# Eight narrow columns of a projection: one wide product per 512 tokens, or strips of 32 columns placed side by side

## The chip, the cores and the metric

The kernel runs on one core of a Trainium2 chip. The metric is the device time of one execution in microseconds. The engines are TensorE (PE in the profile; PEld is its weight load), VectorE (DVE), ScalarE (ACT), GpSimd (POOL) and SyncE (SP), which here issues nearly all DMAs. Each engine runs its own list of instructions in order; semaphores tie the lists together.

## The reference

One layer of a trunk over 2048 tokens of width 1024. The input is normalised and projected to four gated DeltaNet heads and four HGRN2 heads; their outputs are joined, projected, and followed by an MLP and a gated embedding term. What the change touches are eight columns of the projection: `a_gdn` and `b_gdn`, one of each per DeltaNet head.

```
hn = rms_norm(h, pre_mix_norm[i])
proj = jnp.einsum('btd,dc->btc', hn, w_in[i])
a_gdn = proj[..., OFF_GDN_A:OFF_GDN_B]          # 4 columns
b_gdn = proj[..., OFF_GDN_B:OFF_HG_F]           # 4 columns
beta = jax.nn.sigmoid(b_gdn)
g_dec = -jnp.exp(gdn_a_log[i]) * jax.nn.softplus(a_gdn + gdn_dt_bias[i])
o_a = gated_delta_rule_chunked(q_a, k_a, v_a, g_dec, beta)
```

The rule forms running sums of `g_dec` in each chunk and uses their exponentials, so a head needs the sums along the tokens as a row, and the sums and the gates as columns with one token per partition.

## The kernel before, in words

The mixer stage (39 to about 1010 us) works on four quarters of 512 tokens. x is held transposed, as eight tiles of 128 features by 512 tokens (`xt`), each scaled and then split into a high and a low part (`split`: ACT copies the rounded part, DVE subtracts). A product of x with 128 columns of weights, split likewise, is 24 matmuls of 128x128 by 128x512: high by high, high by low, low by high for each of eight k. The list `works` names the products in order. For each quarter it begins with the product `ab`, whose 128 columns hold the eight wanted ones (rows 0 to 3 and 32 to 35 of the result) and otherwise nothing that is used; then come eight products for each of four pairs of heads. `stage_work` loads the weights of a product three works ahead, `split_work` splits them two ahead, `keep_work` stores the split weights to memory in quarter 0, and the later quarters load them from there.

A product is three steps of eight matmuls. After each step a clock ticks, and the generators entered in an agenda (`at(time, generator, offsets)`) run on to their next yield. These issue the mixers' small work: `gdn_mixer` and `hgrn_mixer` of each head, `load_x` (loads, scalings and splits of the next quarter's x, in nine pieces during the nine steps before the boundary), and `decays`. PE's list is thus the program's order with the small matmuls at the ticks, SP's is by hand in the mixer loop, and the lists of ACT, DVE and POOL are set by a scheduler.

`decays` takes the result of `ab`. It evacuates four rows with a bias (L526) and four with a tanh (L527), forms the softplus by Exp and Ln of -|a| (L529 to L532; each of the two functions needs a table load on ACT), scales (L533) and forms the running sums in four scans (L535). It stores the sums to memory (L539), turns their order for odd chunks (L542), and transposes four tiles of 36 rows on PE (L546) into the columns `gcol`. Each DeltaNet head loads its own row of sums into `gf` (L638).

Around a boundary between quarters the list holds the end of the old quarter's heads: the last chunks of DeltaNet's recurrence (`psa` on PE, `r_g` on DVE, `psb` on PE, `w_g` on ACT, `psc` and `of_g` on PE, the new state `S_g` on DVE, and again `psa`), the HGRN head's `qk` on DVE and `hb` on ACT, and the next head's triangular system, a chain of short DVE operations `pr_g` and `xs_g`.

Quarter 0 is special: an embedding stage ahead of it (7 to 39 us) runs products `mme`, squares and their sums, and scales and splits the first x; ACT, DVE and SP have an order by hand there. `rsb_x` is the row of the inverse norms, spread over the partitions by DMA, that this scaling reads.

Of the kernel before, what the change touches and what calls it, by code (L numbers as in the profile page):

```python
# [10 lines left out]
F32 = mybir.dt.float32  # L11
# [4 lines left out]
ALU = mybir.AluOpType  # L16
# [4 lines left out]
P = 128  # L21
# [41 lines left out]
A_AHEAD = (-8, -6)  # L63


A_FIRST = (3, 7, 8, 8, 9, 10, 12, 14) + tuple(range(16, 24)) + (24, 26, 29, 32, 34, 36, 37)

A_LAST = (A_STEPS[:16] + (24, 25, 27, 28, 29, 30, 31) + tuple(range(32, 44))
# [28 lines left out]
def trunk(ctx, tc, x, xT, pT, vecs, w_in, w_ab, gdn_a_log, gdn_dt_bias, w_out, w_up, w_down,  # L97
# [30 lines left out]
    dec = cp.tile([4, 2], F32, name="dec")  # L128
# [15 lines left out]
    nexpa = cp.tile([4, 1], F32, name="nexpa")  # L144

    def vectors():

        ps = bank("ps_rows", pp)
        PE.transpose(ps[:, :N_ROWS], rows, ident[:N_ROWS, :N_ROWS])
        V.tensor_copy(cols, ps[:, :N_ROWS])  # L150
        V.tensor_scalar(ple_w, cols[:, R_PLE : R_PLE + KD], 0.5, None, ALU.mult)
        V.tensor_tensor(lb, lg, lg, ALU.subtract)
        S.activation(lb, lb, AF.Exp)
        V.reciprocal(lb1, lb)
        V.tensor_tensor(lb, lb, lb1, ALU.mult)
        V.tensor_tensor(lb, lb, lb, ALU.subtract)
# [3 lines left out]
        S.activation(nexpa, dec[:, 0:1], AF.Exp)  # L160
        V.tensor_scalar(nexpa, nexpa, -1.0, None, ALU.mult)

    mhalf = cp.tile([P, NC], F32, name="mhalf")
    V.memset(mhalf, -0.5)
# [220 lines left out]
    def half():  # L385

        for gen in agenda.pop(clock[0] - 0.5, ()):
            next(gen, None)

    with ExitStack() as ectx:  # L390
        es = ectx.enter_context(tc.tile_pool(name="es", bufs=1))
        with tc.manual_schedule(engines={mybir.EngineType.SP, mybir.EngineType.Activation, mybir.EngineType.DVE}):
# [9 lines left out]
            nc.sync.dma_start(dec[:, 0:1], gdn_a_log.rearrange("o h -> h o"))  # L402
            nc.sync.dma_start(dec[:, 1:2], gdn_dt_bias.rearrange("o h -> h o"))
# [39 lines left out]
            def put_x():  # L443
                k = len(xts[0])
                xts[0].append(operand(ra, None, f"xt0_{k}", raw=xraw[:, k]))
# [8 lines left out]
                done.append(d)  # L454
            while len(xts[0]) < KD:
                put_x()
            for f in stores:
                f()


    with mixers as mctx:
# [54 lines left out]

            return ready

        gb = mt("gb", "gb", 1, (36, QT))
        V.memset(gb, 0.0)  # L520

        def decays(ps, q):

            sp = m2.tile([4, QT], F32, tag="tmp", name=f"sp_{q}")
            se = m2.tile([4, QT], F32, tag="th", name=f"se_{q}")
            S.activation(sp, ps[0:4, :], AF.Identity, bias=dec[:, 1:2])  # L526
            S.activation(gb[32:36, :], ps[32:36, :], AF.Tanh, scale=0.5)  # L527
            V.tensor_scalar(gb[32:36, :], gb[32:36, :], 0.5, 0.5, ALU.mult, ALU.add)
            V.scalar_tensor_tensor(se, sp, -1.0, sp, ALU.mult, ALU.max)  # L529
            S.activation(se, se, AF.Exp, scale=-1.0)  # L530
            S.activation(se, se, AF.Ln, bias=1.0)
            V.scalar_tensor_tensor(sp, sp, 0.0, se, ALU.max, ALU.add)  # L532
            V.tensor_scalar(sp, sp, nexpa, None, ALU.mult)  # L533
            for c in range(NC):
                V.tensor_tensor_scan(gb[0:4, blk(c)], one[0:4, :], sp[:, blk(c)], 0.0, ALU.mult, ALU.add)  # L535
            gd = dr.tile([4, QT], F32, name=f"gd{q}")
            decay[q] = [gd, None]
            yield
            nc.sync.dma_start(gd, gb[0:4, :])  # L539
            yield  # L540
            back = mt(f"gbb_{q}", "gbb", 1, (36, QT // 2))
            V.tensor_copy(back.rearrange("p (n b i) -> p n b i", b=NB, i=SB), odd_back(gb))  # L542
            yield
            ps = bank(f"ps_gb_{q}", ph)
            for c in range(NC):
                PE.transpose(ps[:, c * 36 : (c + 1) * 36], back[:, blk(c // 2)] if c % 2 else gb[:, blk(c)],  # L546
                             ident[:36, :36])
            gcol = sm.tile([P, NC, 36], F32, tag="gcol", name=f"gcol_{q}", bufs=2)
            V.tensor_copy(gcol.rearrange("p c n -> p (c n)"), ps[:, : NC * 36])
# [83 lines left out]
        def gdn_mixer(q, h, live):  # L633
# [8 lines left out]
            beta = gcol[:, :, 32 + h : 33 + h].rearrange("p c o -> p (c o)")  # L642
            cd = sm.tile([P, NC], F32, tag="cd", name=f"cd_{n}")
            both = sm.tile([P, 2, NC], F32, tag="tail", name=f"tail_{n}")
            tail, eg = both[:, 0], both[:, 1]
# [372 lines left out]
                yield  # L1018
            at(t, once(), (0,))

        STEPS = SPT = 3
# [63 lines left out]
        def load_x(q):  # L1085

            rsb = spread_load(x_r[q], f"x{q}", m2, "rsx", 1)
            raws = {}

            def load(k):  # L1090
                raws[k] = m2.tile([P, QT], F32, tag="ld", name=f"raw_xt{q}_{k}", bufs=2)
                nc.sync.dma_start(raws[k], xT[blk(k), tok(q)])

            def scale(k):
                V.scalar_tensor_tensor(raws[k], raws[k], col(R_PREMIX + k), rsb, ALU.mult, ALU.mult)

            def ready(k):
                t = ra.tile([P, 2, QT], F32R, tag="ring", name=f"xt{q}_{k}")
                split(t, V, raws.pop(k))
                xts[q].append(t)  # L1100

            xts[q] = []
            for k in (0, 1):
                load(k)
            yield
            for k in (2, 4):
                t = wp.tile([P, 2, QT], F32, tag="raw", name=f"raw_xt{q}_{k}", bufs=2)
                nc.sync.dma_start(t, xT[k * P : (k + 2) * P, tok(q)].rearrange("(k p) t -> p k t", p=P))
                raws[k], raws[k + 1] = t[:, 0], t[:, 1]
            for k in (0, 1):  # L1110
                scale(k)
                ready(k)
                load(k + 6)
                yield
            for k in range(2, KD):
                scale(k)
                if k % 2:
                    yield
            for k in range(2, KD):
                ready(k)  # L1120
                if k % 2:
                    yield

        def down_sums(g):

# [14 lines left out]
                for k, n in enumerate(names):  # L1140
                    sumd[n, g] = c, k

        per_q = SPT * (1 + 8 * 4)
        starts = [per_q * q + 5 + n * i for q, m, n in ((1, 6, 14), (2, 5, 16), (3, 5, 16)) for i in range(m)]
        for g, t in enumerate(starts):
            at(t, down_sums(g), (0, 4, 6, 10))
        for q in range(1, NQ):
            at(per_q * (q - 1) + 30, x_scale(q), range(0, 22, 2))
            at(per_q * q, load_x(q), range(-9, 0))
            call(per_q * q, boundary)  # L1150
        for q in range(2):
            at(0, norm_steps(accs[q], 1.0 / D, EPS, f"e{q}", partial(ple_r.__setitem__, q)),
               [4 * q + i for i in (0, 2, 4, 5, 6)])
        with tc.manual_schedule(engines={mybir.EngineType.SP}):
            stage_work(0)
            stage_work(1)
# [3 lines left out]
            for j, (name, key, src, q, h, then, g, b) in enumerate(works):  # L1160
# [9 lines left out]
                for s in range(SPT):  # L1170
                    for i in range(s * nt // SPT, (s + 1) * nt // SPT):
                        if i == (2 * s + 1) * nt // (2 * SPT):
                            half()
                        PE.matmul(ps, *terms[i], start=i == 0, stop=i == nt - 1)  # L1174
                    if s == SPT - 1 and h is None:
                        at(clock[0], decays(ps, q), (0, 2, 3, 5) if q else (0, 2, 4, 7))
                    tick()
                    if s == SPT - 1 and h is not None:
                        then(ps, q, h, g, b)

            outs = early_outs()
# [801 lines left out]
```

## Time and profile before

| | us |
|---|---|
| median of 3 runs (2644.4 to 2645.62) | 2645.34 |
| the profiled execution | 2640.8 |
| its span, from first to last instruction | 2639.0 |
| PE busy in the span | 2602.0 |
| DVE busy | 1964.8 |
| ACT busy | 1466.0 |
| POOL busy | 137.0 |

The granted clock of TensorE was 1.000 throughout. A row of the timeline gives the start, the length, the engine, the line, the operation and its tiles; a square bracket behind it says how long the engine idled before it and which instruction ended the idling. The length of a matmul includes its way through the array, and matmuls overlap, so the distance between starts is their price. In a row of the windows stand, for each engine, the busy time and the count of instructions in that stretch, then the granted clock, the busy share of the DMA engines and the GB/s.

### The profile page before, as it was taken

How to read it: one execution, taken by the hardware profiler on the slowest of the kernel's cores; microseconds unless marked ns; L12 is line 12 of the kernel's file. 1: busy time of each engine (PE TensorE's matmuls, PEld its weight loads, DVE VectorE, ACT ScalarE, POOL GpSimd, SP SyncE). 2: the span in 40 equal slices, each digit the busy share in tenths (PEclk: the TensorE clock that was granted, in tenths of full speed). 3: DMA queues.
4: the chain of work that ended last, by engine and by line, in shares of the span. 5: the costliest groups of instructions: out<-in, count | busy, mean ns of one | idle time of the engine just before them, and what ended most of it. 6: DMA issues, size and time to landing. Idle time of an engine off the chain costs nothing.

```text
span 2639.0 us, 43910 instructions
## 1 busy us (share of the span) xinstructions
PE 2602.0 (99%) x15593; PEld 2143.6 (81%) x15593; DVE 1964.8 (74%) x4032; ACT 1466.0 (56%) x2991; POOL 137.0 (5%) x147
## 2 busy tenths in 40 slices
PE   8999999999999999999999999999999999999999
PEld 6787788878878888787888888888888888888887
DVE  7778777776777777579988778767877765478775
ACT  7665655465556555566666465555454465565331
POOL 0000000000000000110000000001000001101000
PEclk9999999999999999999999999999999999999999
DMA  8878777767767675774675576665644475677663
GB/s 279 288 243 263 255 270 247 239 221 248 244 201 251 224 235 163 225 214 138 215 234 183 179 234 224 213 212 186 224 145 168 140 245 186 202 252 251 209 219 128
DMA packets 267788, 573.87 MB, mean 217 GB/s; under 512 B 55578, under 2 KB 60152, under 8 KB 250416
## 3 DMA queue, kind: packets, MB, share of 16 engines
q1 hardware_dynamic: 265264, 566.86, 65.0%
q0 software_dynamic: 2304, 4.20, 0.9%
q8 instruction: 123, 2.02, 0.3%
q14 instruction: 97, 0.79, 0.1%
HBM read 410.57 MB, written 160.37 MB: 216 GB/s over the span
## 4 chain that ended last, share of the span: by engine, by line
PE 80%; DVE 7%; DMA 6%; ACT 3%; issue 3%; SPq 1%; POOL 0%; DVEq 0%; ACTq 0%; POOLq 0%
PE d L1208 23%; PE u L1208 23%; PE mm L1174 19%; PE mmg L1208 7%; PE mmo L1057 1%; PE mme L203 1%; DMA xs<-in_x_dram 1%; DMA ud_g<-u_g 1%; DMA cache_in<-w 1%; DMA sys_g<-ud_g 1%; DVE pr_g L744 1%; DVE xs_g L746 0%; DMA wd<-in_w_down_dram 0%; DVE xt L177 0%; PE psc_g L828 0%
## 5 line engine op out<-in xcount | busy, mean ns | idle before, releaser
L1174 PE MATMUL mm<-xt,w 128*128 128x512 f32 x3072 | 786.4, 401 | 2.9 <-DVE acc_vg L569 1.5
L1174 PEld LDWEIGHTS mm<-xt,w 128*128 128x128 f32 x3072 | 552.9, 188 | 109.0 <-ACT w L176 1.9
L1208 PE MATMUL d<-db,da 128*128 128x512 f32 x2688 | 612.9, 389 | 0.0
L1208 PE MATMUL u<-t,wu 128*128 128x512 f32 x2604 | 591.2, 389 | 0.0
L1208 PEld LDWEIGHTS d<-db,da 128*128 128x128 f32 x2688 | 504.5, 188 | 104.7
L1208 PEld LDWEIGHTS u<-t,wu 128*128 128x128 f32 x2604 | 488.8, 188 | 101.5
L230 DVE TENSOR_TENSOR db<-db 128x512 fp32r<-128x512 f32 x224 | 159.5, 712 | 60.6 <-ACT db L229 60.2
L1606 DVE TENSOR_TENSOR u<-u,u 128x512 f32<-128x512 f32 x224 | 150.0, 680 | 52.4 <-PE u L1208 50.9
L229 ACT ACTIVATE db<-db 128x512 fp32r<-128x512 f32 x224 | 141.0, 629 | 65.3 <-DMA db<-hid 60.8
L1208 PE MATMUL mmg<-h2T,wg 128*128 128x512 f32 (+1 forms) x792 | 174.7, 383 | 0.0
L1208 PEld LDWEIGHTS mmg<-h2T,wg 128*128 128x128 f32 x792 | 145.5, 188 | 29.1
L1649 ACT ACTIVATE u<-u 128x512 f32<-128x512 f32 x128 | 80.7, 631 | 152.8 <-DVE u L1606 152.2
L177 DVE TENSOR_TENSOR da<-da 128x512 fp32r<-128x512 f32 x128 | 93.9, 734 | 91.6 <-ACT da L176 91.3
L176 ACT ACTIVATE da<-da 128x512 fp32r<-128x512 f32 x128 | 80.6, 630 | 128.3 <-DMA da<-sumd 110.2
L1208 PE MATMUL mmo<-mixT,w_out 128*128 128x512 f32 x600 | 138.7, 391 | 3.3 <-DVE w_out L177 2.0
L1208 PEld LDWEIGHTS mmo<-mixT,w_out 128*128 128x128 f32 x600 | 112.2, 188 | 28.8 <-DVE w_out L177 3.2
L176 ACT ACTIVATE wu<-a 128x512 fp32r<-128x512 f32 x124 | 75.1, 623 | 54.8 <-DMA a<-in_w_up_dram 51.8
L177 DVE TENSOR_TENSOR wu<-a,wu 128x512 fp32r<-128x512 f32 x124 | 85.7, 694 | 8.8 <-ACT wu L176 8.3
L177 DVE TENSOR_TENSOR da<-dr,da 128x512 fp32r<-128x512 f32 x96 | 68.2, 711 | 22.5 <-ACT da L176 20.9
L1650 ACT ACTIVATE u<-u 128x512 f32<-128x512 f32 x128 | 80.4, 628 | 3.0
L176 ACT ACTIVATE da<-dr 128x512 fp32r<-128x512 f32 x96 | 60.5, 630 | 31.4 <-DMA dr<-in_w_down_dram 25.6
L246 POOL TENSOR_TENSOR acc_y<-acc_y,sq_y 128x512 f32<-128x512 f32 x28 | 37.8, 1349 | 759.4 <-ACT sq_y L245 759.4
(402 smaller groups left out, 3673.3 us busy)
## 6 DMA issues: line engine op xcount, KB each, us to landing
w<-cache_in SPq DMA_DIRECT2D x96, 1024.0 KB
db<-hid SPq DMA_DIRECT2D x224, 256.0 KB
cache_in<-w SPq DMA_DIRECT2D x32, 1024.0 KB
hid<-u SPq DMA_DIRECT2D x128, 256.0 KB
da<-sumd SPq DMA_DIRECT2D x128, 256.0 KB
a<-in_w_up_dram SPq DMA_DIRECT2D x124, 256.0 KB
hid<-ht SPq DMA_DIRECT2D x96, 256.0 KB
dr<-in_w_down_dram SPq DMA_DIRECT2D x96, 256.0 KB
```

The costliest lines, as they stand in the source:

```text
L176: S.activation(t[:, 0], raw, AF.Copy)
L177: eng.tensor_tensor(t[:, 1], raw, t[:, 0], ALU.subtract)
L203: PE.matmul(ps, a, b, start=i == 0, stop=i == n - 1)
L229: S.activation(t[:, 0], plain(t), AF.Copy)
L230: V.tensor_tensor(t[:, 1], plain(t), t[:, 0], ALU.subtract)
L246: eng.tensor_tensor(acc, acc, sq, ALU.add)
L744: V.tensor_tensor(pr[:, :, :, j + 2 :], xs[:, :, None, j + 2 :].broadcast_to([P, GC, 2, i]), sys[:, None, j : j + 2, j + 2 :].broadcast_to ...
L1174: PE.matmul(ps, *terms[i], start=i == 0, stop=i == nt - 1)
L1208: PE.matmul(ps, a, b, start=start, stop=stop)
L1606: V.tensor_tensor(c[new], c[old], ps, ALU.add)
L1649: S.activation(c[k], c[k], AF.Relu)
L1650: S.activation(c[k], c[k], AF.Square)
```

## The change

The work `ab` goes, with its loads, splits, stores and reloads. The eight columns of weights are loaded once (`few`, 36 columns of each k), copied by POOL into a small tile `w_few` of eight columns per k, and kept. For each quarter `few_columns` issues fp32 matmuls of 32 columns of weights by 128 tokens: the four groups of 128 tokens go to the four column positions of the array, so that the result is one tile of 128x128, in which strip c holds tokens 128c to 128c+127, decays in rows 0 to 3 and gates in rows 4 to 7 of each strip. In quarter 0 the moving side is the scaled, unsplit x of eight k; later it is the unsplit x for k = 2 to 7, and the high and the low part for k = 0 and 1, whose unsplit tiles are no longer kept.

`decays` works on tiles of 128x128 then. A column `sign` turns the gates' rows, and sigmoid(b) is taken as exp(-softplus(-b)), so that a third table load and one more Exp replace the tanh. There is one scan instead of four; the sums are stored so that a head's row of 512 is contiguous; POOL makes two copies in turned order, and PE transposes four tiles of 128x128. The steps at which `decays` advances are `FEW_STEPS` (in quarter 0 `FEW_FIRST`), counted from the strips, and `load_x` begins two steps earlier (`X_STEPS`). A quarter has 96 steps instead of 99.

```diff
+FEW_FIRST = (0, 2, 5)
+FEW_STEPS = (0.5, 2, 4)
+X_STEPS = (-11, -10, -9, -7, -6, -5, -3, -2, -1)
...
+    def few_columns(q, terms):
+        ps = bank(f"few_{q}", pp)[:, :P]
+        for i, (k, x) in enumerate(terms):
+            for c in range(NC):
+                PE.matmul(ps[c * SB : (c + 1) * SB, :], w_few[:, k * 8 : k * 8 + SB], x[:, blk(c)], start=i == 0,
+                          stop=i == len(terms) - 1, tile_position=(0, c * SB), skip_group_check=True)
+        return ps
...
+            few = es.tile([P, KD, 36], F32, name="few")
+            nc.sync.dma_start(few, w_ab[:, :, :36])
+            for c in range(1, NC):
+                G.tensor_copy(dec[c * SB : c * SB + 4, :], dec[:4, :])
+            for i in range(2):
+                G.tensor_copy(w_few[:, : KD * 8].rearrange("p (k n) -> p k n", n=8)[:, :, 4 * i : 4 * i + 4],
+                              few[:, :, 32 * i : 32 * i + 4])
...
+            few_first = few_columns(0, [(k, xraw[:, k]) for k in range(KD)])
...
         def decays(ps, q):
-            sp = m2.tile([4, QT], F32, tag="tmp", name=f"sp_{q}")
-            se = m2.tile([4, QT], F32, tag="th", name=f"se_{q}")
-            S.activation(sp, ps[0:4, :], AF.Identity, bias=dec[:, 1:2])
-            S.activation(gb[32:36, :], ps[32:36, :], AF.Tanh, scale=0.5)
-            V.tensor_scalar(gb[32:36, :], gb[32:36, :], 0.5, 0.5, ALU.mult, ALU.add)
+            sp, se, sums, beta = (mt(f"{n}_{q}", n, 1, (P, P)) for n in ("gsp", "gse", "gsum", "gbeta"))
+            S.activation(sp, ps, AF.Identity, scale=sign, bias=dec[:, 1:2])
             V.scalar_tensor_tensor(se, sp, -1.0, sp, ALU.mult, ALU.max)
             S.activation(se, se, AF.Exp, scale=-1.0)
             S.activation(se, se, AF.Ln, bias=1.0)
             V.scalar_tensor_tensor(sp, sp, 0.0, se, ALU.max, ALU.add)
+            S.activation(beta, sp, AF.Exp, scale=-1.0)
             V.tensor_scalar(sp, sp, nexpa, None, ALU.mult)
-            for c in range(NC):
-                V.tensor_tensor_scan(gb[0:4, blk(c)], one[0:4, :], sp[:, blk(c)], 0.0, ALU.mult, ALU.add)
+            V.tensor_tensor_scan(sums, one, sp, 0.0, ALU.mult, ALU.add)
...
+            nc.sync.dma_start(gd.rearrange("r (c t) -> c r t", t=P), sums)
...
+            for i, t in enumerate((sums, beta)):
+                back = mt(f"back_{i}_{q}", f"back{i}", 1, (P, P))
+                G.tensor_copy(back.rearrange("p (b i) -> p b i", i=SB), t.rearrange("p (b i) -> p b i", i=SB)[:, ::-1])
+                PE.transpose(turns[:, i, 0], t, ident)
+                PE.transpose(turns[:, i, 1], back, ident)
...
+            halves = [(k, xts[q][k].bitcast(F32)[:, i, :]) for k in (0, 1) for i in range(2)]
+            at(clock[0], decays(few_columns(q, halves + [(k, raws[k]) for k in range(2, KD)]), q), FEW_STEPS)
...
-            works.append((f"ab{q}", "ab", w_ab, q, None, None, None, None))
...
-        per_q = SPT * (1 + 8 * 4)
+        per_q = SPT * 8 * 4
...
-            at(per_q * q, load_x(q), range(-9, 0))
+            at(per_q * q, load_x(q), X_STEPS)
```

How the lists move. First ACT at the boundary into quarter 1, before and after (`zt_gh` belongs to the old quarter's last product, `w_g_2_2` to the recurrence of its third DeltaNet head, `gsp`, `gse` and `gbeta` to `decays`):

```order
L604 ACTIVATE zt_gh_3_3459<-mm_0_3_3376 128x512
L825 ACTIVATE w_g_2_2_3470<-psb_g_2_2_3468,cc_g_2_1794 128x128
L286 ACTIVATE osq_h_2_3418<-nrm_h_2_3476 1x512
L880 ACTIVATE hb_h_3_3485<-qk_h_3_3196 128x256
L526 ACTIVATE sp_3536<-mm_ab_3463,dec 4x512
L527 ACTIVATE gb<-mm_ab_3463 4x512
L530 ACT_TABLE_LOAD
L530 ACTIVATE se_3537<-se_3537 4x512
```

```order
L627 ACTIVATE zt_gh_3_3513<-mm_0_3_3389 128x512
L548 ACTIVATE gsp_3526<-few_3472,dec,sign 128x128
L903 ACTIVATE hb_h_3_3552<-qk_h_3_3225 128x256
L550 ACT_TABLE_LOAD
L550 ACTIVATE gse_3527<-gse_3527 128x128
L848 ACTIVATE w_g_2_2_3524<-psb_g_2_2_3522,cc_g_2_1801 128x128
L551 ACT_TABLE_LOAD
L551 ACTIVATE gse_3527<-gse_3527 128x128
L288 ACTIVATE osq_h_2_3431<-nrm_h_2_3543 1x512
L553 ACT_TABLE_LOAD
L553 ACTIVATE gbeta_3529<-gsp_3526 128x128
```

`w_g_2_2` stood directly behind `zt_gh`; it now stands behind `gsp`, `hb`, a table load and `gse`. In quarter 3 `hb` stands behind `gbeta` instead.

DVE at the same place, before and after, from the product `qk` on:

```order
L878 TENSOR_TENSOR qk_h_3_3196<-qk_h_3_3196,gg_h_3_0_3486 128x2x128
L830 SCALAR_TENSOR_TENSOR S_g_2_2_3506<-S_g_2_1_3383,cd_g_2_1788,psc_g_2_2_3504 128x128
L937 TENSOR_TENSOR gg_h_3_6_3982<-gg_h_3_5_3906 128x4
L727 COPY pr_g_0_4098<-cst 128x4x16
L930 TENSOR_TENSOR qk_h_3_3196<-qk_h_3_3196,gg_h_3_0_3486 128x2x64x2
L820 SCALAR_TENSOR_TENSOR r_g_2_3_3524<-psa_g_2_3_3522,tail_g_2_1789,vt_g_2_2491 128x128
L529 SCALAR_TENSOR_TENSOR se_3537<-sp_3536 4x512
```

```order
L901 TENSOR_TENSOR qk_h_3_3225<-qk_h_3_3225,gg_h_3_0_3553 128x2x128
L549 SCALAR_TENSOR_TENSOR gse_3527<-gsp_3526 128x128
L953 TENSOR_TENSOR qk_h_3_3225<-qk_h_3_3225,gg_h_3_0_3553 128x2x64x2
L552 SCALAR_TENSOR_TENSOR gsp_3526<-gsp_3526,gse_3527 128x128
L853 SCALAR_TENSOR_TENSOR S_g_2_2_3573<-S_g_2_1_3396,cd_g_2_1795,psc_g_2_2_3571 128x128
L554 TENSOR_SCALAR gsp_3526<-gsp_3526,nexpa 128x128
L555 SCALAR_TENSOR_TENSOR gsum_3528<-one,gsp_3526 128x128
L843 SCALAR_TENSOR_TENSOR r_g_2_3_3592<-psa_g_2_3_3590,tail_g_2_1796,vt_g_2_2491 128x128
```

`S_g_2_2` and `r_g_2_3` stood ahead of all of `decays`; the state now stands behind the softplus's last step (L552), and `r_g_2_3` behind the scan as well.

SP in the embedding stage, before and after (`raw_...` are loads of weights for the first products, `rsb_x` the spread inverse norms):

```order
L410 DMA xraw<-in_xT_dram 128x2x512 x2
L252 DMA rd_x_375<-ss_x_294 128x4
L510 DMA raw_ab_614<-in_w_ab_dram 128x1024
L257 DMA rsb_x_377<-rd_x_375 128x512
L410 DMA xraw<-in_xT_dram 128x2x512 x2
```

```order
L430 DMA xraw<-in_xT_dram 128x2x512 x2
L531 DMA raw_0_0_658<-in_w_in_dram 128x1024
L254 DMA rd_x_384<-ss_x_305 128x4
L531 DMA raw_0_0_660<-in_w_in_dram 128x1024
L259 DMA rsb_x_386<-rd_x_384 128x512
L430 DMA xraw<-in_xT_dram 128x2x512 x2
```

`rsb_x` now stands behind a second load of weights, which must wait for a buffer that an earlier split releases.

More of the change, by code (lines that the diff above doesn't have):

```diff
@@ L127, in trunk @@
     rows = cp.tile([N_ROWS, P], F32, name="rows")
-    dec = cp.tile([4, 2], F32, name="dec")
+    dec = cp.tile([P, 2], F32, name="dec")
+    w_few = cp.tile([P, KD * 8 + SB - 8], F32, name="w_few")
     ident = cst[:, C_IDENT, :]
@@ L143, in trunk @@
     lb, lb1, ha, hna, hb = (bounds[:, i] for i in range(5))
-    nexpa = cp.tile([4, 1], F32, name="nexpa")
+    nexpa, sign = (cp.tile([P, 1], F32, name=n) for n in ("nexpa", "sign"))
     def vectors():
@@ L159, in vectors @@
         V.tensor_tensor(hb, lb, ha, ALU.add)
-        S.activation(nexpa, dec[:, 0:1], AF.Exp)
-        V.tensor_scalar(nexpa, nexpa, -1.0, None, ALU.mult)
     mhalf = cp.tile([P, NC], F32, name="mhalf")
@@ L401, in trunk @@
             nc.sync.dma_start(rows, vecs)
-            nc.sync.dma_start(dec[:, 0:1], gdn_a_log.rearrange("o h -> h o"))
-            nc.sync.dma_start(dec[:, 1:2], gdn_dt_bias.rearrange("o h -> h o"))
+            G.memset(dec, 0.0)
+            G.memset(w_few, 0.0)
+            nc.sync.dma_start(dec[:4, 0:1], gdn_a_log.rearrange("o h -> h o"))
+            nc.sync.dma_start(dec[:4, 1:2], gdn_dt_bias.rearrange("o h -> h o"))
+            few = es.tile([P, KD, 36], F32, name="few")
[5 more added lines that the diff above has]
+                              few[:, :, 32 * i : 32 * i + 4])
             nc.sync.dma_start(praw[1], pT[:, tok(1)].rearrange("(k p) t -> p k t", p=P))
@@ L517, in stage @@
             return ready
-        gb = mt("gb", "gb", 1, (36, QT))
-        V.memset(gb, 0.0)
+        S.activation(nexpa, dec[:, 0:1], AF.Exp)
+        V.tensor_scalar(nexpa, nexpa, -1.0, None, ALU.mult)
+        V.tensor_reduce(sign, ident.rearrange("p (c n) -> p c n", n=SB)[:, :, 4:8], AX.XY, ALU.add)
+        V.tensor_scalar(sign, sign, -2.0, 1.0, ALU.mult, ALU.add)
         def decays(ps, q):
-            sp = m2.tile([4, QT], F32, tag="tmp", name=f"sp_{q}")
-            se = m2.tile([4, QT], F32, tag="th", name=f"se_{q}")
-            S.activation(sp, ps[0:4, :], AF.Identity, bias=dec[:, 1:2])
-            S.activation(gb[32:36, :], ps[32:36, :], AF.Tanh, scale=0.5)
-            V.tensor_scalar(gb[32:36, :], gb[32:36, :], 0.5, 0.5, ALU.mult, ALU.add)
+            sp, se, sums, beta = (mt(f"{n}_{q}", n, 1, (P, P)) for n in ("gsp", "gse", "gsum", "gbeta"))
+            S.activation(sp, ps, AF.Identity, scale=sign, bias=dec[:, 1:2])
             V.scalar_tensor_tensor(se, sp, -1.0, sp, ALU.mult, ALU.max)
@@ L641, in gdn_mixer @@
             gc = gcol[:, :, h : h + 1].rearrange("p c o -> p (c o)")
-            beta = gcol[:, :, 32 + h : 33 + h].rearrange("p c o -> p (c o)")
+            beta = gcol[:, :, 8 + h : 9 + h].rearrange("p c o -> p (c o)")
             cd = sm.tile([P, NC], F32, tag="cd", name=f"cd_{n}")
@@ L1019, in call @@
             at(t, once(), (0,))
-        STEPS = SPT = 3
+        SPT = 3
         for q in range(NQ):
-            works.append((f"ab{q}", "ab", w_ab, q, None, None, None, None))
             for h in range(4):
@@ L1098, in ready @@
                 t = ra.tile([P, 2, QT], F32R, tag="ring", name=f"xt{q}_{k}")
-                split(t, V, raws.pop(k))
+                split(t, V, raws[k])
                 xts[q].append(t)
@@ L1120, in load_x @@
                 ready(k)
-                if k % 2:
+                if k % 2 and k + 1 < KD:
                     yield
+            halves = [(k, xts[q][k].bitcast(F32)[:, i, :]) for k in (0, 1) for i in range(2)]
+            at(clock[0], decays(few_columns(q, halves + [(k, raws[k]) for k in range(2, KD)]), q), FEW_STEPS)
+            yield
         def down_sums(g):
@@ L1153, in trunk @@
                [4 * q + i for i in (0, 2, 4, 5, 6)])
+        at(0, decays(few_first, 0), FEW_FIRST)
         with tc.manual_schedule(engines={mybir.EngineType.SP}):
@@ L1174, in trunk @@
                         PE.matmul(ps, *terms[i], start=i == 0, stop=i == nt - 1)
-                    if s == SPT - 1 and h is None:
-                        at(clock[0], decays(ps, q), (0, 2, 3, 5) if q else (0, 2, 4, 7))
                     tick()
-                    if s == SPT - 1 and h is not None:
+                    if s == SPT - 1:
                         then(ps, q, h, g, b)
```

17 lines of the change are left out of this document (7 added, 10 removed).

## The prediction

> **What bounds the kernel now.** First the page: the span, the busy shares, the chain that ended last.
>
> ```profile
> span 2639.0 us, 43910 instructions
> ...
> PE 2602.0 (99%) x15593; PEld 2143.6 (81%) x15593; DVE 1964.8 (74%) x4032; ACT 1466.0 (56%) x2991; POOL 137.0 (5%) x147
> ...
> PE 80%; DVE 7%; DMA 6%; ACT 3%; issue 3%; SPq 1%; POOL 0%; DVEq 0%; ACTq 0%; POOLq 0%
> ```
>
> TensorE (PE) is busy 2602.0 of 2639.0 us, so work taken from it shortens the span unless a new wait fills the hole. The question is therefore what PE waits for at the four places where the decay product stood. The groups of instructions, and PE's timeline at the first of these places and at the second (the boundary into quarter 1):
>
> ```profile
> L1174 PE MATMUL mm_ab<-xt,w_ab 128*128 128x512 f32 x96 | 24.5, 397 | 0.2 <-ACT sq_e L245 0.2
> ```
>
> ```profile
> 38.91 5.74 PE L1174 MATMUL mm_ab<-xt,w_ab 128*128 128x512 f32 x24 [0.19 <-ACT sq_e L245]
> ...
> 275.64 1.08 PE L1174 MATMUL mm_ab<-xt,w_ab 128*128 128x512 f32 x4
> 276.56 0.39 PE L823 MATMUL psb_g<-r_g,xt_full 128*128 128x128 f32 x2
> ...
> 279.06 0.39 PE L828 MATMUL psc_g<-w_g,kt_g 128*128 128x128 f32 x2
> 279.28 0.39 PE L831 MATMUL of_g<-y_qg,S_g 128*128 128x128 f32 x2
> ```
>
> Matmuls overlap, so a price is the distance between starts: four wide ones take 276.56 - 275.64 = 0.92 us, 0.23 each. The 96 of the decay product are 96 x 0.23 = 22.1 us of PE's path, 5.5 per quarter. They ran almost unbroken (0.2 us idle), but with small matmuls of two mixers between them (psb, psc), whose operands come from ScalarE (ACT) and VectorE (DVE). How full those two are at the boundaries, from the windows (columns: PE, PEld, DVE, ACT, POOL, granted clock, DMA):
>
> ```profile
> 255.00:260.00 5.00, 5.00 (x32) 4.37 (x31) 3.82 (x19) 2.15 (x7) 0.00 (x0) 1.00 1.01 327
> 260.00:265.00 5.00, 5.00 (x29) 4.33 (x28) 4.26 (x15) 1.44 (x4) 0.00 (x0) 1.00 0.95 305
> ...
> 275.00:280.00 5.00, 5.00 (x28) 4.28 (x27) 5.00 (x14) 1.73 (x4) 0.00 (x0) 1.00 0.49 120
> ...
> 285.00:290.00 5.00, 5.00 (x64) 4.07 (x64) 1.04 (x3) 3.30 (x6) 0.00 (x0) 1.00 0.60 210
> ```
>
> DVE has no free time from 275 to 280, but 1.9 us free in 255 to 265 and 4.0 in 285 to 290. So DVE is the engine on which a shorter boundary can run aground, and ACT, half idle by share, counts through its order alone.
>
> **The change, part by part.**
>
> *The product goes: -22.1 us.*
>
> *The strips come.* 32 matmuls of 32 columns by 128 tokens in quarter 0 (8 terms x 4 positions) and 40 in each other quarter (10 terms). The kernel has such strips already:
>
> ```profile
> 65.81 1.52 PE L1174 MATMUL mm<-xt,w 128*128 128x512 f32 x6
> 67.27 0.49 PE L631 MATMUL of_g<-y_kg 128*32 128x128 f32 x16
> ...
> 68.11 0.47 PE L631 MATMUL of_h<-y_kg 128*32 128x128 f32 x16
> 68.40 0.47 PE L631 MATMUL of_h<-y_qg,y_kg 128*32 128x128 f32 x16
> 68.79 3.49 PE L1174 MATMUL mm<-xt,w 128*128 128x512 f32 x14
> ```
>
> Each such group is eight strips (two records each): by the code widths 128, 96, 64 and 32 twice, 160 columns at each of the four positions. It takes 0.29 us (68.11 to 68.40) or 0.39 (to 68.79). A term of the new strips has 128 columns per position: 0.29 x 128/160 = 0.23 us, at most 0.31. Quarter 0: 8 x 0.23 = 1.9; the others 10 x 0.23 = 2.3 each; together 8.8 us (11.8 at the upper price). If the four positions did not overlap at all, a strip would cost what a 128-wide unsplit matmul does (279.06 to 279.28, 0.22 us): 0.88 per term. I take 0.23, since the same form of strip is in the rows. The Trainium skill (TensorEngine Tiling (Array Packing), Key Properties) says that a change of tiling mode drains TensorE. Here the six wide matmuls ahead of the strips take 1.46 us where 6 x 0.23 = 1.38, so a switch shows at most 0.08 us; eight switches would take 0.6 us from the gain.
>
> *The transposes.* Four of 36 columns become four of 128:
>
> ```profile
> 541.13 0.25 PE L546 MATMUL ps_gb<-cst,gb 36*128 36x36 f32 x1
> ...
> 541.50 1.70 PEld L1174 LDWEIGHTS mm<-xt,w 128*128 128x128 f32 x8
> ```
>
> ```profile
> 766.50 0.60 PE L599 MATMUL t_ih<-cst,iT_h 128*128 128x128 f32 x4
> 766.85 2.09 PE L1174 MATMUL mm<-xt,w 128*128 128x512 f32 x8
> ```
>
> 0.37 us against 0.35: nothing. PE alone therefore gives 22.1 - 8.8 = 13.3 us: 3.6 in quarter 0 and 3.2 at each boundary.
>
> *The new order on ACT at a boundary.* The rows of ACT and DVE at quarter 1:
>
> ```profile
> 276.98 0.37 ACT L825 ACTIVATE w_g<-psb_g,cc_g 128x128 f32<-128x128 f32 x1 [0.54 <-PE psb_g L823]
> ...
> 282.33 0.43 ACT L880 ACTIVATE hb_h<-qk_h 128x256 f32<-128x256 f32 x1 [3.39 <-DVE qk_h L878]
> ...
> 283.36 0.59 ACT L527 ACTIVATE gb<-mm_ab 4x512 f32<-4x512 f32 x1
> 283.97 1.28 ACT L530 ACT_TABLE_LOAD   x1
> 285.26 0.63 ACT L530 ACTIVATE se<-se 4x512 f32<-4x512 f32 x1
> ```
>
> ```profile
> 275.87 0.34 DVE L820 SCALAR_TENSOR_TENSOR r_g<-psa_g,tail_g,vt_g 128x128 f32<-128x128 f32 x1
> ...
> 277.26 0.68 DVE L177 TENSOR_TENSOR xt<-raw_xt,xt 128x512 fp32r<-128x512 f32 x1
> ...
> 281.88 0.41 DVE L878 TENSOR_TENSOR qk_h<-qk_h,gg_h 128x256 f32<-128x256 f32 x1
> ...
> 288.96 0.68 DVE L532 SCALAR_TENSOR_TENSOR sp<-sp,se 4x512 f32<-4x512 f32 x1 [4.44 <-ACT se L531]
> ...
> 290.63 1.35 DVE L535 TENSOR_TENSOR_SCAN gb<-one,sp 4x128 f32<-4x128 f32 x4
> ```
>
> Before, w_g followed its psb at once (276.98) and PE's psc at 279.06 found it. Now ACT runs gsp, hb (which waits for DVE's qk), a table load, the Exp gse, and only then w_g. PE reaches psc at 275.64 + 2.3 (strips) + 12 x 0.23 + 0.6 (psb and two norm matmuls) = 281.3. From r_g to qk DVE took 6.0 us; without the one qk step now ahead of r_g, 5.3. The scaling of x is moved up to two steps (3.7 us) earlier, towards the 1.9 us free before 265; I let r_g come 0.9 us earlier, at 275.0. Then qk ends at 280.6, hb at 281.0, the load at 282.3, gse (128 wide, as w_g 0.37) and w_g at 283.0: PE waits 1.7 us. If DVE is 1.9 us ahead the wait is near 0.7, and with the table loaded before hb none; if it is not ahead at all (r_g as before plus the qk step's 0.4), it is 3.1, the whole saving. I take 1.7, and 1.5 net.
>
> ```profile
> 500.00:505.00 5.00, 5.00 (x32) 4.37 (x31) 2.74 (x12) 1.99 (x6) 0.00 (x0) 1.00 1.03 326
> ```
>
> ```profile
> 750.00:755.00 5.00, 4.09 (x22) 3.21 (x20) 2.64 (x14) 1.59 (x6) 0.00 (x0) 1.00 0.96 331
> ```
>
> Ahead of quarters 2 and 3 DVE has 2.3 us free in one window, and in quarter 3 hb comes after w_g: waits of 1.1 and 0.7, net 2.1 and 2.5. Behind it DVE's S_g now queues behind the second half of the softplus: w_g 283.0, load 1.28, Ln 0.37, two DVE steps of 0.34 give S_g at 285.4, and PE wants it for psa at 283.0 + 0.6 + 12 x 0.23 = 286.4: 1.0 us to spare. The transposes, 8 matmuls later (288.5), need the third load, beta's Exp and a GpSimd (POOL) copy: 284.7 + 0.6 (osq) + 1.28 + 0.4 + 0.3 = 287.3, again in time. DVE itself sheds work (scan 1.35 becomes one 128-wide pass near 0.34; 0.68 becomes 0.34), covered by its idle 4.44 us.
>
> The Trainium skill (ScalarE: Activation LUTs, What ACT_TABLE_LOAD costs) puts a switch of tables at 2.66 us with a drain. By that each boundary would lose 1.4 us more, 4.1 in all. The trace disagrees: the load at 283.97 begins 0.02 us after the activation ahead of it, and the next starts 0.01 after its 1.28 us.
>
> *Quarter 0.* The strips have no load of w_ab, but the first head product's weights are loaded and split inside the embedding stage, and SP's queue holds the second such load ahead of rsb_x:
>
> ```profile
> 18.92 0.33 SPq L257 DMA_DIRECT2D rsb_x<-rd_x  x1
> ```
>
> ```profile
> 14.39 1.02 POOL L172 TENSOR_TENSOR ss_x<-ss_x,mhalf 128x4 f32<-128x4 f32 x1 [13.95 <-DVE ss_x L424]
> ```
>
> ```profile
> 20.29 1.29 DVE L177 TENSOR_TENSOR w_plea<-raw_plea,w_plea 128x512 fp32r<-128x512 f32 x2
> 23.36 1.23 DVE L177 TENSOR_TENSOR w_ab<-raw_ab,w_ab 128x1024 fp32r<-128x1024 f32 x1 [1.78 <-ACT w_ab L176]
> ...
> 25.11 0.74 DVE L441 SCALAR_TENSOR_TENSOR xraw<-xraw,cols,rsb_x 128x512 f32<-128x512 f32 x1
> ```
>
> That load waits for the buffer that w_plea's split frees at 21.6, so rsb_x issues 2.7 us later, against a scaling at 25.11 that had no wait. DVE is full there to 38 us, and one more split costs 1.23. I take 2.1 of the 3.6 as lost, 1.5 kept; bounds: 1.23 + 2.7 lost (-0.3) and nothing lost (3.6). The small DMAs for the 36 columns and POOL's copies into w_few stand around POOL's one operation of that stage (14.39), more than 20 us ahead of the strips; I cost them at nothing, and 0.3 us for a late SP queue is inside the bounds. Loads, stores and reloads of w_ab (1 MB each) go; no PE row waited for them.
>
> Sum: 1.5 + 1.5 + 2.1 + 2.5 = 7.6 us. The profiled execution took 2640.8 us, 1.8 over its span, and lies 4.5 under the median of 2645.34. 2640.8 - 7.6 = 2633.2, and by the median 2637.7.
>
> **Rivals.** (a) No new wait: all 13.3 us come through, 2632. For it speaks that DVE idles 4 us right behind the boundary, against it the order on ACT. (b) The waits eat it: 3.1 us at each boundary and a prologue that loses 3.9 leave 13.3 - 9.3 - 3.9 = 0.1, 2645. For it speaks DVE's 5.00 of 5.00; it decides once the waits exceed 8 us in all. (c) Slower: the four positions do not overlap when each accumulates over 8 or 10 terms. 152 strips x 0.22 = 33.4 us against 22.1: 11.3 slower, and w_g then comes in time: 2657. It decides from 22.1/38 = 0.58 us per term. Against it stand the 0.29 us groups. (d) Slower by displaced work: the earlier steps of x crowd the heads before the boundary, where PE now has no wait; it needs a loss of 2 us per boundary beyond (b): about 2651.
>
> **How the numbers follow.** A measurement of this kernel tells about 0.2%, 5.3 us. Forecast (gain 5.3 to 11): 0.52; (a) 0.10; (b) 0.23; (c) 0.05; (d) 0.10. Faster 0.62, same 0.23, slower 0.15. The range from 2630 (more than (a)) to 2651 (d) leaves out (c) and part of (d). The forecast's own range is 2634 to 2640.
>
> **What would show it.** PE's groups: no mm_ab, strips at 1.9 to 3.1 us per quarter; L1200's first product within 2.5 us of the strips' start. PE's waits: psc for w_g, 1 to 2 us at quarter 1, less later. DVE's wait for rsb_x in the prologue, and the first head product some 1.5 us ahead of the old product's end (38.91 + 5.74). Wrong would be: strips over 0.4 us per term; a wait of PE at psa, ps_gb or on a split of x; or waits at the later heads that the old trace did not have.

## The result and the profile after

The changed kernel takes 2695.7 us (2688.77 to 2698.94, 4 runs) against 2644.87 (4 runs): 1.0181 times as long, 95% interval 1.0166 to 1.0197. The forecast was 2638, and 2651 was the end of its range. The page after, span and busy shares:

```profile
span 2691.2 us, 44339 instructions
...
PE 2637.4 (98%) x15801; PEld 2144.3 (80%) x15801; DVE 1956.0 (73%) x4016; ACT 1468.0 (55%) x2996; POOL 141.9 (5%) x162
```

PE is busy 35 us longer, although a net 13 us of matmuls left. What the change itself put on PE came as forecast. PE's timeline at quarter 1, and the transposes behind it:

```profile
279.71 1.08 PE L397 MATMUL few<-xt,w_few 128*32 128x128 f32 x32
280.61 1.49 PE L397 MATMUL few<-raw_xt,w_few 128*32 128x128 f32 x48
282.03 1.19 PE L1200 MATMUL mm<-xt,w 128*128 128x512 f32 x4
...
287.81 0.80 PE L851 MATMUL psc_g<-w_g,kt_g 128*128 128x128 f32 x2 [2.04 <-ACT w_g L848]
...
294.98 0.27 PE L566 MATMUL ps_gb<-cst,gsum 128*128 128x128 f32 x1
...
295.34 1.17 PE L1200 MATMUL mm<-xt,w 128*128 128x512 f32 x4
```

The strips take 282.03 - 279.71 = 2.32 us, the four transposes 0.36, and PE waits 2.04 us for w_g. ACT's timeline at the same place:

```profile
285.45 0.43 ACT L903 ACTIVATE hb_h<-qk_h 128x256 f32<-128x256 f32 x1 [2.82 <-DVE qk_h L901]
285.90 1.28 ACT L550 ACT_TABLE_LOAD   x1
287.19 0.31 ACT L550 ACTIVATE gse<-gse 128x128 f32<-128x128 f32 x1
287.41 0.35 ACT L848 ACTIVATE w_g<-psb_g,cc_g 128x128 f32<-128x128 f32 x1
```

The loss lies elsewhere. First, in the MLP, which the change does not touch. The windows of 1300 to 1900 us, where PE never idles, before and after (first numbers: PE's busy time and its matmuls):

```profile
1300.00:1900.00 600.00, 600.00 (x2649) 496.87 (x2648) 469.61 (x735) 335.31 (x556) 19.36 (x14) 1.00 0.64 210
```

```profile
1300.00:1900.00 600.00, 600.00 (x2603) 488.83 (x2602) 463.64 (x726) 328.87 (x546) 19.22 (x14) 1.00 0.62 204
```

In the same 600 us PE starts 2603 matmuls instead of 2649, at a granted clock of 1.00 in both: each takes 1.8% longer. Second, in waits. PE's waits before and after:

```profile
PE psc_g L828 <- ACT w_g L825: 1.9, 3, 0.9
...
PE psa_g L818 <- DVE S_g L830: 1.1, 2, 0.6
```

```profile
PE psc_g L851 <- ACT w_g L848: 14.2, 12, 2.6
...
PE psa_g L841 <- DVE S_g L853: 4.4, 5, 1.1
PE mm L1200 <- ACT zt_zg L627: 3.8, 1, 3.8
PE psb_g L846 <- DVE r_g L843: 3.2, 3, 2.7
```

Few of these 21 stand at a boundary; most are in mid-quarter. Third, in stretches at half the clock. The windows behind the wait at quarter 1:

```profile
286.00:288.00 2.00, 0.18 (x1) 0.19 (x2) 0.34 (x1) 1.97 (x4) 0.00 (x0) 0.92 0.67 283
288.00:290.00 2.00, 2.00 (x8) 1.90 (x9) 0.55 (x2) 1.97 (x4) 0.00 (x0) 0.50 0.44 66
290.00:292.00 2.00, 2.00 (x8) 1.53 (x8) 0.45 (x2) 1.47 (x2) 0.29 (x1) 0.72 0.80 328
```

The column after POOL's is the granted clock: 0.50 for 3.4 us after the wait. The record of the clock holds five such stretches inside the changed kernel, four of 3.4 us and one of 10.2 at quarter 2, and before none until the last microsecond; at half the clock 23.9 us lose up to 12. Not all of that is the change's. The first stretch, at 21.45 us, follows a wait of 2.24 us in the embedding stage, and the kernel before has the same wait (2.26 us). Other executions of the kernel before have mean granted clocks of 0.996 to 1.000, those of the changed kernel 0.995 to 0.997.

### The profile page after: what moved, and what is told of

It reads as the page before. It is cut to its first block, busy times and chain, and to the rows that moved or that the text cites. A ratio compares the mean times of both kernels' runs of the same rounds, so it can differ in the third digit from the quotient of the medians.

```text
span 2691.2 us, 44339 instructions
## 1 busy us (share of the span) xinstructions
PE 2637.4 (98%) x15801; PEld 2144.3 (80%) x15801; DVE 1956.0 (73%) x4016; ACT 1468.0 (55%) x2996; POOL 141.9 (5%) x162
## 4 chain that ended last, share of the span: by engine, by line
PE 55%; DVE 2%; DMA 2%; issue 2%; ACT 1%; POOL 0%; SPq 0%; DVEq 0%; POOLq 0%; ACTq 0%
PE u L1232 23%; PE d L1232 22%; PE mmg L1232 7%; PE mmo L1079 1%; PE mme L205 1%; DMA mixT<-mixd 0%; DMA yo<-in_xT_dram 0%; DVE t L179 0%; DVE acc_o L248 0%; DMA rsb_g<-rd_g 0%; POOL yo L1318 0%; DMA raw_out<-in_w_out_dram 0%; DMA yod<-yo 0%; DMA rg<-in_w_gate_dram 0%; DVE w_out L179 0%
## 5 line engine op out<-in xcount | busy, mean ns | idle before, releaser
L1200 PE MATMUL mm<-xt,w 128*128 128x512 f32 x3072 | 802.7, 406 | 6.0 <-ACT zt_zg L627 3.8
L1232 PE MATMUL d<-db,da 128*128 128x512 f32 x2688 | 621.1, 392 | 0.0
L1232 PE MATMUL u<-t,wu 128*128 128x512 f32 x2604 | 604.0, 394 | 0.0
```

Source lines behind the costliest of these rows:

```text
L1232: PE.matmul(ps, a, b, start=start, stop=stop)
```

## A first reading: addresses

PE's list of wide matmuls (10344 before, 10248 in the changed kernel) can be laid beside the built program, which knows the address of each operand. In the kernel before, the moving tile and the weights of every wide matmul lie a multiple of 256 bytes apart. The change adds 384 bytes per partition to the pool of small constants (w_few 352, the column `sign` 32 with its rounding), and takes 768 from a pool behind it (the narrower `gcol`). The tiles of x so move up by 384 and the MLP's tiles down by 384, while the weights of the mixers and part of the MLP's operands, taken from the other end of the memory, stay. Distances of 0 become 128 modulo 256. The distance between two starts, by that difference (pairs under 300 ns apart, so without waits):

| kernel | difference mod 256 | matmuls | mean ns | median |
|---|---|---|---|---|
| before, mixers | 0 | 2520 | 228.5 | 227 |
| before, the rest | 0 | 7068 | 226.8 | 227 |
| changed, mixers | 128 | 2417 | 232.5 | 232 |
| changed, the rest | 128 | 4615 | 232.6 | 232 |
| changed, the rest | 0 | 2454 | 227.9 | 227 |

The last two rows stand in one execution. It is not the addresses by themselves: of the last row, 777 matmuls have both operands at 96 modulo 256, where all operands of the kernel before lie at 224, and they too start 227 ns apart (median). Theory: matmuls whose operands differ by 128 start 5.3 ns later each. Rival: a lasting throttle, set off by the strips or the new waits.

## The experiments

**Addresses.** An unused tile of 128 bytes brings all distances of the changed kernel back to 0:

```diff
+    cp.tile([P, 32], F32, name="fill")
     dec = cp.tile([P, 2], F32, name="dec")
```

> The changed kernel with one unused tile of 32 floats (128 bytes per partition) ahead of the small constant tiles, so that the tiles of x and of the MLP lie 128 bytes further on; nothing that is computed changes. Address theory: in the changed kernel 7776 of 10248 wide matmuls have a moving tile whose address differs from that of the weights by 128 modulo 256, and these start 232.5 ns apart where the others start 227 apart. With the filler none differs, so the distance returns to 227 ns in the mixers and in the MLP, and the time falls by 7776 x 5.3 ns = 41 us, from 2695.7 to 2650 to 2660 us; what is left against before is the waits and the half-clock stretches. Rival, a throttle set off by the new waits (or by the strips) that slows TensorE for the rest of the run: the filler changes nothing, 2689 to 2699 us and 232 ns.

Measured: 2666.36 us, 1.0059 (1.0046 to 1.0072) of the kernel before on the same chip, 2649.09. Its MLP window:

```profile
1300.00:1900.00 600.00, 600.00 (x2649) 496.99 (x2648) 472.94 (x741) 334.71 (x557) 19.14 (x14) 1.00 0.63 208
```

2649 matmuls again, as before. From 1.0181 to 1.0059 is 32 us, of the 41 expected; what became of the other 9 no run shows. The converse, in the kernel before: the same filler with 128 bytes less padding (mixers off, most of the MLP kept), and less padding alone (MLP off):

```diff
+    cp.tile([P, 32], F32, name="fill")
...
-    ctx.enter_context(tc.tile_pool(name="pad", bufs=1)).tile([P, 48], F32, name="pad")
+    ctx.enter_context(tc.tile_pool(name="pad", bufs=1)).tile([P, 16], F32, name="pad")
```

> The kernel before with the same filler of 128 bytes, and 128 bytes less of padding ahead of the MLP's tiles, which so stay where they were. Now 4842 matmuls (the mixers' and, by way of the tiles of x, 1530 of the others) have operands 128 apart modulo 256. Address theory: 4842 x 5.3 ns = 26 us slower, 2668 to 2675 us, with 232 ns in the mixer stage and 227 in most of the MLP. Rival (throttle or strips): 2645 us, no change.

> The kernel before with 128 bytes less of padding ahead of the MLP's tiles and no other edit: 3630 matmuls have operands 128 apart modulo 256, all but 48 of them behind the mixers. Address theory: 3630 x 5.3 ns = 19 us slower, 2660 to 2667 us; mixers at 227 ns as before. Rival: 2645 us.

Measured: 2661.66 us, 1.0043 (1.0028 to 1.0058), and 2670.62 us, 1.0075 (1.0061 to 1.0089). The groups of the mixers' products, first of mixers off, then of MLP off (401 ns before), and the MLP windows of both in the same order:

```profile
L1175 PE MATMUL mm<-xt,w 128*128 128x512 f32 x3072 | 796.1, 404 | 2.2 <-DVE w L178 1.2 <-ACT w L177 0.7 <-DMA w<-cache_in 0.3
```

```profile
L1174 PE MATMUL mm<-xt,w 128*128 128x512 f32 x3072 | 787.3, 401 | 2.0 <-DVE acc_vg L569 1.4 <-DVE w L177 0.6
```

```profile
1300.00:1900.00 600.00, 600.00 (x2631) 493.55 (x2630) 466.93 (x730) 330.22 (x550) 19.31 (x14) 1.00 0.63 208
```

```profile
1300.00:1900.00 600.00, 600.00 (x2606) 488.92 (x2605) 460.98 (x720) 326.85 (x543) 19.21 (x14) 1.00 0.62 204
```

Each stage slows where its own distances were spoilt (the 2631 between the two is from the 1530 matmuls that read tiles of x's pool there), by 12.6 and 21.5 us for 26 and 19 expected. Between starts, the mixers' matmuls take 232.4 ns on average in the first of these kernels and 228.6 in the second, as before. Why the first loses only half of what its count of matmuls gives, no run shows. No strip is in these kernels, so neither strips nor a throttle of theirs is needed. Which other distances are slow was looked at with padding of 32 and of 40 floats:

> The kernel before with 64 bytes less of padding ahead of the MLP's tiles: the same 3630 matmuls have operands 64 or 192 apart modulo 256. If only a distance of 0 modulo 256 is fast: about 19 us slower, 232 ns. If a distance of 64 is as good as 0: 2645 us, 227 ns. Rival without addresses: 2645 us.

> The kernel before with 32 bytes less of padding ahead of the MLP's tiles: the same 3630 matmuls as in the runs off by 128 and 64 bytes have operands 32 or 224 apart modulo 256. If only a distance of 0 is fast: 232 to 234 ns and about 20 to 27 us slower, as at 64. If what counts is a multiple of 32: 227 ns and no change.

Measured, one time each: 2675.29 and 2667.61 us beside 2649.09 and 2646.53, with 2604 and 2606 matmuls in the MLP window. Differences of 64 and 192 give 232.5 and 233.3 ns, of 32 and 224 give 233.2 and 233.4. Among the distances tried (0, 32, 64, 128, 192, 224) only 0 modulo 256 is fast. The weights of the next matmul count too: 82 matmuls of the changed kernel have their own two operands 0 apart, but lie 128 from the weights of the matmul behind them. They take 232.7 ns, and the same 82 in the kernel with the filler 227.3. What collides inside the chip no run shows.

**The agenda.** With the filler 17 us remained. At quarter 2 of that kernel SP, DVE and PE read:

```profile
507.07 1.52 SPq L1165 DMA_DIRECT2D sumd<-wd  x2
508.63 1.04 SPq L260 DMA_DIRECT2D rsb_x<-rd_x  x1
509.72 1.68 SPq L1115 DMA_DIRECT2D raw_xt<-in_xT_dram  x2
```

```profile
517.96 0.75 DVE L1118 SCALAR_TENSOR_TENSOR raw_xt<-raw_xt,cols,rsb_x 128x512 f32<-128x512 f32 x1 [5.05 <-DMA raw_xt<-in_xT_dram]
...
522.78 0.34 DVE L844 SCALAR_TENSOR_TENSOR r_g<-psa_g,tail_g,vt_g 128x128 f32<-128x128 f32 x1
```

```profile
523.18 0.80 PE L847 MATMUL psb_g<-r_g,xt_full 128*128 128x128 f32 x2 [3.62 <-DVE r_g L844]
```

Before, in SP's timeline, the same stores and loads stood at:

```profile
484.50 1.16 SPq L1139 DMA_DIRECT2D sumd<-wd  x2
...
499.79 0.98 SPq L1092 DMA_DIRECT2D raw_xt<-in_xT_dram  x2
```

`down_sums` and `x_scale` are entered at offsets from a quarter's start (5 and 30). Before, the heads began 3 steps into the quarter, behind the decay product; now they begin at its start, so these two are 3 steps late against them. The store of `sumd` stands 22.6 us later, in an execution that is by then some 9 us behind; rsb_x and the loads of x follow it directly in SP's queue, DVE waits 5.05 us for x with r_g behind it, and PE waits for r_g. The store is not the whole of this wait. The loads of x are 9.9 us later than before, where PE's products are 8.6, so they are late by 1.3 us. Before, DVE scaled x only at 508.56, 8.8 us behind the load, and worked on the next head's system (pr_g, xs_g) until then; now the scaling stands ahead of that work in its list. The edit puts both entries back:

```diff
-        starts = [per_q * q + 5 + n * i for q, m, n in ...
+        starts = [per_q * q + 2 + n * i for q, m, n in ...
-            at(per_q * (q - 1) + 30, x_scale(q), range(0, 22, 2))
+            at(per_q * (q - 1) + 27, x_scale(q), range(0, 22, 2))
```

> The changed kernel with the filler, and the two entries of the agenda that are counted from the start of a quarter and not from its heads (the sums of w_down's blocks, offset 5, and the norms of the next quarter's x, offset 30) put 3 steps earlier, where they stood against the heads before the change. Theory A: without the three steps of the decay product these two came 3 steps late against the heads; their work on DVE and their buffers then met the heads' starts and the load of x (TensorE's waits at psc in mid-quarter, 1.0 to 2.6 us each, and 3.6 us plus a half-clock stretch at quarter 2 where x was late). Then those waits go, and the time falls by 10 to 17 us against the filler alone, to between 0.995 and 1.002 of before. Rival B, the mid-quarter waits come from the lists that the scheduler wrote for the new decays: they stay, ratio 1.004 to 1.008.

Measured: 2648.77 us, 1.0002 (0.9992 to 1.0013): 15 us gone. The wait of 3.62 us at psb is gone too; another, of 3.25 us at psa for S_g, stands at the same boundary, and psc still waits 10.6 us for w_g in all (14.7 with the filler alone). The converse is the kernel before with these offsets 3 later (8 and 33):

> The kernel before with the two entries of the agenda 3 steps later (offsets 8 and 33), all else as it was, the decay product included. Theory A: the same waits arise without strips and without the filler; 8 to 17 us slower than before, waits at psc in mid-quarter and around the boundaries. Rival B: within 3 us of before.

Measured: 2659.39 us, 1.0040 (1.0025 to 1.0055), 10.5 us slower, with the same waits in a kernel that has no strips:

```profile
PE psc_g L828 <- ACT w_g L825: 8.3, 6, 2.9
PE psa_g L818 <- DVE S_g L830: 5.2, 5, 2.5
```

So rival B of these runs falls as the account of the 15 us. It does not fall for the waits at psc that stayed, which theory A expected to go. Two edits beside it, the decays one step later and x in the nine steps of before:

> As the run with the agenda moved, and the decays' steps after the strips one step later (1.5, 3, 5 for 0.5, 2, 4). On ACT w_g then stands ahead of the first table load at quarters 2 and 3, at quarter 1 still behind it. Theory A with the forecast's boundary wait: 1 to 3 us faster than without (TensorE's waits for w_g at the last two boundaries gone, the one of about 2 us at quarter 1 left). Rival: the transposes ps_gb are late in their place and nothing is gained, within 1 us.

> As the run with the agenda moved, and the load of x in nine consecutive steps from the ninth before the boundary, as before the change. If the earlier start of x was needed: waits of TensorE on splits of x or on r_g around the boundaries, 2 to 6 us slower than with the earlier steps. If it only displaced other work: equal or up to 3 us faster.

Measured: 1.0007 (0.9994 to 1.0019), no gain where 1 to 3 us were expected; and 2648.40 in one time, no change that can be told. A wait of 3.3 to 3.9 us for zt_zg at 74 us was in all of them. ACT ahead of it, in the kernel with the filler alone and before:

```profile
62.90 1.28 ACT L671 ACT_TABLE_LOAD   x1
...
65.78 1.28 ACT L602 ACT_TABLE_LOAD   x1 [1.37 <-DVE tail_g L672]
...
67.72 1.28 ACT L674 ACT_TABLE_LOAD   x1
...
72.97 1.28 ACT L628 ACT_TABLE_LOAD   x1
74.26 0.60 ACT L628 ACTIVATE zt_zg<-mm 128x512 f32<-128x512 f32 x1
```

```profile
62.32 1.28 ACT L647 ACT_TABLE_LOAD   x1
...
65.83 1.28 ACT L578 ACT_TABLE_LOAD   x1
...
69.66 0.64 ACT L604 ACTIVATE zt_zg<-mm 128x512 f32<-128x512 f32 x1
```

Two loads more, because the first head's Exp work is torn apart: its tail_g on DVE comes late. A third entry of the agenda also counts from step 0, the norms of the embedding, whose steps fall among the first head's now. It went 3 steps earlier too (not below 0), with x in nine steps:

```diff
-               [4 * q + i for i in (0, 2, 4, 5, 6)])
+               [max(4 * q + i - 3, 0) for i in (0, 2, 4, 5, 6)])
```

> The changed kernel with the filler, all three entries of the agenda that count from a quarter's start put 3 steps earlier (the sums of w_down, the norms of x, and now also the norms of the embedding in quarter 0, not below step 0), and x loaded from the ninth step on. On ACT in quarter 0 the first head's Exp work stands together again, with one table load less ahead of zt_zg's product. Theory A (late agenda): TensorE's wait of 3.3 to 3.9 us for zt_zg at 74 us goes, and with it the half-clock stretch behind it: 4 to 5 us faster than the run with the agenda moved and x from the ninth step, 0.998 to 0.999 of before. Rival: the first head is late for the strips' decays themselves (three tables, POOL's copies), and the wait stays.

> As the run with all three entries moved, and the decays one step later (1.5, 3, 5): on ACT w_g stands ahead of the table load at all three boundaries. Forecast's mechanism: the waits at psc of 1 to 2 us behind the boundaries go, 1 to 4 us faster than without, down to 0.9965 of before. Rival: other waits at the boundary take their place, no change.

> The changed kernel with the filler and all three entries of the agenda 3 steps earlier, and the changed kernel's own steps for x (from the eleventh before the boundary). If the earlier steps of x matter for nothing but the collision already undone: within 2 us of the run with nine steps, 0.998 to 1.000 of before. If they crowd the heads ahead of the boundary: 2 to 4 us slower than it.

Measured: 0.9993 (0.9985 to 1.0001), 0.9999 (0.9991 to 1.0008) and, with the changed kernel's own steps for x, 0.9991 (0.9981 to 1.0002) at 2644.30 us. In each the wait for zt_zg is gone, and it is worth some 2 us, not the 4 to 5 expected. The decays one step later bring nothing here either, where 1 to 4 us were expected: in that trace PE waits 6.9 us for w_g instead of 7.9, and 4.2 us for r_g at psb instead of 0.4. So the rival of that run holds. The last is the best version found, some 2 us ahead of before, which its interval does not quite tell from nothing. What PE still waits for there:

```profile
PE psc_g L852 <- ACT w_g L849: 8.4, 9, 2.0
PE psa_g L842 <- DVE S_g L854: 5.5, 4, 3.8
```

## Why the prediction failed, point by point

- **The strips' price** held: 2.32 us at quarters 1 to 3 for 2.3, and 44.94 - 43.06 = 1.88 in quarter 0 for 1.9. Rival (c), positions that do not overlap, falls. The transposes held (0.36 us).
- **The wait for w_g at quarter 1** held: 2.04 us for 1.7, by the mechanism named. r_g did not come earlier (279.72, at the strips' start), and qk, hb, the load and gse followed in the chain forecast. PE for its part reached psc 6.06 us behind the strips' start, not 5.66, so two errors partly cancel. Behind the wait came 3.4 us at half the clock, for which the forecast had no term. The table load again ends where the next activation begins (285.90 + 1.28 = 287.18, next at 287.19), so the drain that the Trainium skill (ScalarE: Activation LUTs, What ACT_TABLE_LOAD costs) counts was rightly left out.
- **Quarters 2 and 3**: the waits forecast there, 1.1 and 0.7 us at the psc behind the strips, did not come. That psc follows the matmul ahead of it without a wait (first two rows). Others came some 15 us ahead of the strips, while x was loaded: 2.72 us at psb for r_g (third row) and 1.07 at psa for S_g.

```profile
544.85 0.40 PE L851 MATMUL psc_g<-w_g,kt_g 128*128 128x128 f32 x2
...
795.54 0.38 PE L851 MATMUL psc_g<-w_g,kt_g 128*128 128x128 f32 x2
```

```profile
523.85 0.80 PE L846 MATMUL psb_g<-r_g,xt_full 128*128 128x128 f32 x2 [2.72 <-DVE r_g L843]
```

Quarter 2's wait was another than the one forecast: x was late. The forecast counted the earlier steps of x as a help to DVE and did not ask whether SP's queue would let the loads go.
- **Quarter 0**: the step kept at most 0.5 us, not 1.5. The timeline of SP, DVE and PE:

```profile
22.37 0.38 SPq L259 DMA_DIRECT2D rsb_x<-rd_x  x1
```

```profile
28.22 0.75 DVE L461 SCALAR_TENSOR_TENSOR xraw<-xraw,cols,rsb_x 128x512 f32<-128x512 f32 x1 [0.74 <-DMA rsb_x<-rd_x]
```

```profile
43.06 1.95 PE L397 MATMUL few<-xraw,w_few 128*32 128x128 f32 x64
44.94 3.30 PE L1200 MATMUL mm<-xt,w 128*128 128x512 f32 x13
```

rsb_x is 3.5 us late as described, the scaling at 28.22 follows, and the first head product starts at 44.94, where it started at 45.45 before. But before, two norm matmuls (nrm_e, from 44.48) stood ahead of it, and they now stand behind it (50.64), so by the work done nothing is kept. Part of that may be chance, through the half-clock stretch at 21.45. The 3.8 us for zt_zg were not foreseen.
- **The step that failed** is the sum itself, "22.1 - 8.8 = 13.3" with 0.23 us for a wide matmul and nothing for the stages untouched. It took a duration read before the change as a property of the instruction. Two new tiles and a narrower one changed the distance between the operands of 7776 matmuls, and that cost 32 us by the filler's ratio (1.0181 to 1.0059). None of the rivals had a term for it either.
- **The second missing term** is the agenda: "a quarter has 96 steps instead of 99" stood in the description of the change, and no step asked what else counts from a quarter's start. Two entries cost 15 us (1.0059 to 1.0002), in part through half-clock stretches behind the longer waits; the third perhaps 2 more (1.0002 to 0.9991, intervals overlapping).
- **What is left** is a gain of some 2 us where 7.6 was the forecast. PE's waits for w_g and S_g (8.4 and 5.5 us, against 1.9 and 1.1 before) can account for most of the 13.3 us. These are sums of one trace each, and the wait for w_g comes to 3.5 to 5.0 us in the three kernels that differ from before in the MLP's padding alone. With that reserve rival (b), waits that eat the saving, describes the mended kernel, and rival (d), displaced work, the mechanism of the agenda, though through other entries than the one it named. Why psc waits in mid-quarter also with the agenda mended is not settled: its lists are the scheduler's, and no run changed one of them alone.

## What to carry to other kernels

A change that adds or resizes a tile moves the operands of work it never touches: compare the addresses of the operands of the main matmuls before and after, and restore their distance with an unused tile. When steps are taken out of a schedule, look for everything that is counted from the point before them, and move it along. A wait is worth more than its length where it sets the clock back.

## What the runs showed of the hardware

A 128x512 fp32r matmul starts every 227 ns when its moving operand and its weights lie 0 modulo 256 bytes apart, and every 232 to 234 ns at 32, 64, 128, 192 and 224, at full granted clock, in the MLP, and for 128 in the mixers too. Waits of PE can be followed by a stretch at half the clock of 3.4 us, or 10.2 where the work behind the wait stays broken. In the windows of the kernel with the filler at quarter 2:

```profile
520.00:522.00 2.00, 0.00 (x0) 0.00 (x0) 0.95 (x3) 0.58 (x1) 0.00 (x0) 0.89 1.02 307
522.00:524.00 2.00, 0.82 (x3) 0.82 (x4) 2.00 (x8) 0.00 (x0) 0.00 (x0) 0.50 1.02 286
524.00:526.00 2.00, 2.00 (x7) 1.61 (x7) 2.00 (x8) 0.65 (x3) 0.00 (x0) 0.50 0.93 382
```

The Trainium skill (TensorE: Matmul & The Clock Gate, Why this matters for your kernels) advises no idle gap above about 3 us between bursts of matmuls. The stretches of 3.4 us agree with the window that page gives (What's actually happening), 3413 ns; but a gap of 2.04 us was enough at quarter 1 of the changed kernel.

The length of one gap is not what decides. Within each of the 14 traces all changes of the clock lie on one grid of 3413 ns, to 5 ns. Cut a trace into these windows and add up PE's idle time in each, leaving out the last 20 us. All 39 windows at full clock with 1.9 us of idle time or more were followed by one at half, 11 of the 34 with 1.45 to 1.87 us, and none of those with less. At half the clock, the 50 windows with at most 0.58 us were followed by full clock and the 6 with 0.63 us or more were not, which is how a stretch grows to 10.2 us. So the same wait can cost nothing when the grid cuts it in two: the 2.26 us in the embedding stage before left 1.54 and 1.02 us of idle time in two windows.
